# Seven products of half blocks in place of eight for 12 of 22 gate and up pairs of a decoder trunk

## The chip, the cores and the metric

The kernel runs on one NeuronCore of a Trainium2 chip. The metric is the device time of one execution in microseconds. Besides the time, one execution was recorded by the hardware profiler; durations below are from that recording.

## The reference

The reference is a trunk of two layers (DEPTH = 2) on x of 512 tokens by 1024 features, in float32. Each layer does, with an RMSNorm ahead of each step:

```
x = x + 0.5 * swiglu(rmsnorm(x, ffn1_norm), ffn1_w_gate_up, ffn1_w_down)
x = x + mixing(rmsnorm(x, mix_norm))     # sparse attention and a spatial gating unit, gated and merged
x = x + 0.5 * swiglu(rmsnorm(x, ffn2_norm), ffn2_w_gate_up, ffn2_w_down)

def swiglu(h, w_gate_up, w_down):
    g, u = split(h @ w_gate_up, 2)       # 1024 -> 2 * 2816
    return (silu(g) * u) @ w_down        # 2816 -> 1024
```

A last RMSNorm follows. So there are four feed-forward stages (FFN) and two mixing stages. In each FFN the gate and the up matrix have 22 blocks of 128 columns each; a gate block and the up block beside it are called a pair.

## The kernel before

**Number format.** Every product is made of three matmuls on float32r operands: a value is split into hi (rounded by ScalarE, `act(hi, src, Copy)`) and lo = value - hi (VectorE), and hi·hi, hi·lo and lo·hi are summed in PSUM. `split` (line 309) is these two instructions. The activations of a stage lie as xh and xl, eight blocks of 128 features by 512 tokens each; a weight tile of 128 x 1024 holds the eight 128 x 128 blocks of one output block.

**FFN** (`ffn`, line 415). The 22 pairs are worked in chunks of 8, 8 and 6 (`CHUNKS`). For each of the two blocks of a pair, `stage` loads a weight tile of 512 KB, splits it into whi and wlo, and `chain` (line 339) issues 24 matmuls of 512 columns into one PSUM bank: for each k the two with the hi weight, and the one with the lo weight one step later (LAG = 1). So a pair has 48 matmuls. Then VectorE multiplies gate and up by the row factor rbc of the norm, ScalarE does Silu, GpSimd multiplies the two, and the result h is split into two of the R tiles. After each chunk the down projection runs over the chunk: for each of eight output blocks dd a weight tile (1024 or 768 columns), a chain of 3 matmuls per pair, and x is updated by VectorE. In the last chunk `norm_prep` prepares the next stage's xh, xl and the sum of squares (which GpSimd adds up for the blocks below 6).

**Buffers.** A ring of a tag holds n tiles; tile number i of a tag takes place i mod n. Weights go through raw (3 tiles), whi (3) and wlo (2); t has 3 tiles. Gate and up results use six of the eight PSUM banks in turn, down results the banks 6 and 7.

**Order.** Every instruction is first noted with its operands, and `order` (line 206) then lists them for each engine: at each step the engine that is free earliest takes, of the instructions that are ready by a table of costs, the one with the smallest number. Loads and splits of weights are noted with a number smaller by AHEAD = 100, so they go ahead of results. The engines then run their lists strictly in that order, with semaphores for the waits. The table knows nothing of one engine slowing another. All DMAs are issued by SyncE. Since all instructions are issued in one line (L259), rows are told apart by tiles: `b<-xh,whi` is a matmul into a bank with moving operand xh and weight whi.

Of the kernel before, what the change touches and what calls it, by code (L numbers as in the profile page):

```python
# [17 lines left out]
P = 128  # L18
S = 512
# [3 lines left out]
NG = (3 * DEPTH + 1) * KD  # L23
CHUNKS = ((0, 8), (8, 16), (16, 22))
LAG = 1
AHEAD = 100
NEG = -1e30
EPS = 1e-6
# [11 lines left out]
class View:  # L40


    def __init__(self, buf, steps, ids, parts, dtype):
        self.buf, self.steps, self.ids, self.parts, self.dtype = buf, steps, ids, parts, dtype
        self.gen = buf.gen

# [88 lines left out]
class Recorder:  # L135
    def __init__(self, nc):
        self.nc, self.ops, self.rings, self.bias, self.ahead = nc, [], {}, {}, 0
        self.real = {"PE": nc.tensor, "DVE": nc.vector, "ACT": nc.scalar, "POOL": nc.gpsimd, "SP": nc.sync}

    def ring(self, tag, n, cols, dtype=F32, psum=False):  # L140
        self.rings[tag] = [[Buffer(f"{tag}_{k}", cols, dtype, psum) for k in range(n)], 0]

    def tile(self, tag, shape):

        bufs, n = self.rings[tag]
        self.rings[tag][1] += 1
# [10 lines left out]
        v = View(b, tuple(steps), _np.arange(cols).reshape(shape[1:]), (0, P), b.dtype)  # L157
        return v if shape[0] == P else v[0:shape[0]]

    def note(self, engine, op, args, kw):  # L160
        outs = [v for v in [args[0], kw.get("accum_out")] if isinstance(v, View)]
        ins = [v for v in list(args[1:]) + [v for k, v in kw.items() if k != "accum_out"] if isinstance(v, View)]
        i, deps = len(self.ops), set()
        for v, writes in [(v, False) for v in ins] + [(v, True) for v in outs]:
            assert v.gen == v.buf.gen, v.buf.name
# [84 lines left out]
    def issue(self, sbuf, psum):  # L250
        for tag, (bufs, _) in self.rings.items():
            for b in bufs:
                if b.log:
                    b.ap = (psum if b.psum else sbuf).tile([P, b.cols], b.dtype, tag=b.name, name=b.name)
# [8 lines left out]
def trunk(ctx: ExitStack, tc, d):  # L263
# [3 lines left out]
    for tag, n, cols in (("cst", 1, C_END), ("gains", 1, NG), ("pes", 1, 32), ("sgub", 1, DEPTH * 8),  # L267
                         ("ones", 1, P), ("x", 1, KD * S), ("rbc", 1, S), ("eps", 1, 1), ("U", 1, NT * S),
                         ("YA", 1, NT * S), ("GN", 1, NT * 24), ("raw", 3, 1024), ("t", 3, S), ("tb", 2, S),
                         ("ga", 4, S), ("pA", 4, S), ("pB", 4, S), ("pc", 1, 256), ("rcol", 2, 4), ("rhalf", 1, 4), ("ss", 1, 4), ("rv", 1, 4), ("sm4", 8, 4), ("sm8", 4, 8)):  # L270
        rec.ring(tag, n, cols)
    for tag, n, cols in (("whi", 3, 1024), ("wlo", 2, 1024), ("VH", 1, NT * S), ("VL", 1, NT * S), ("kc", 1, P),
                         ("vc", 1, 2 * P), ("diagh", 1, S), ("diagl", 1, S)):
        rec.ring(tag, n, cols, F32R)
    for k in range(24):
        rec.ring(f"R{k}", 1, S, F32R)
# [6 lines left out]
    cst, gains, sgub, ones, rbc, eps = (  # L283
        rec.tile(t, [P, rec.rings[t][0][0].cols]) for t in ("cst", "gains", "sgub", "ones", "rbc", "eps"))
    x = rec.tile("x", [P, KD, S])
    pool.memset(ones, 1.0)
    pool.memset(eps, EPS)

    diag = [rec.tile("diagh", [P, S]), rec.tile("diagl", [P, S])]
    for t in diag:  # L290
        pool.memset(t.bitcast(F32), 0.0)
    ident = cst[:, C_ID:C_ID + P]
# [23 lines left out]
    def stage(src, n, mask=None):  # L316
        if first:
            return first.pop(0)
        return load(src, n, mask)

    def load(src, n, mask=None):
        raw, hi, lo = (rec.tile(t, [P, 1024]) for t in ("raw", "whi", "wlo"))
        rec.ahead = AHEAD
# [26 lines left out]

    st = {}

    def norm_begin(gidx):
        st["g"] = gains[:, gidx * KD:(gidx + 1) * KD]
        st["xh"], st["xl"] = [None] * KD, [None] * KD
        st["s"] = None

    def norm_square(k):

        if st["s"] is None:  # L360
            st["s"] = rec.tile("ga", [P, S])
            act(st["s"], x[:, k, :], AF.Square)
# [46 lines left out]
    def norm_finish(b):  # L409
# [3 lines left out]
        return rcol  # L413

    def ffn(gu, dn, l, gnext):
        norm_finish(7)
        xh, xl = st["xh"], st["xl"]
        nb = 0
        for c0, c1 in CHUNKS:
            hh, hl = [], []  # L420
            for j in range(c0, c1):
                bk = []
                for s in range(2):
                    wh, wl = stage(gu[l, 2 * j + s], 1024)
                    ps = bank(nb % 6, "ps_gu")
                    nb += 1
                    chain(ps, [(wh[:, c], wl[:, c], xh[k], xl[k]) for k, c in enumerate(cols(KD))])
                    bk.append(ps)
                g, u = tt("g"), tt("u")
                vec.tensor_tensor(g, bk[0], rbc, op=ALU.mult)  # L430
                act(g, g, AF.Silu)
                vec.tensor_tensor(u, bk[1], rbc, op=ALU.mult)
                pool.tensor_tensor(u, u, g, op=ALU.mult)
                h = rt(2 * (j % 11), "hh")
                lo = rt(2 * (j % 11) + 1, "hl")
                split(h, lo, u)
                hh.append(h)
                hl.append(lo)
# [72 lines left out]

    def mix(l, gnext):
        rcol = norm_finish(7)
        rhalf = rec.tile("rhalf", [P, 4])
        vec.tensor_scalar(rhalf, rcol, 0.5, None, op0=ALU.mult)
# [386 lines left out]
        def filler():  # L902
            for dd in range(4):
                ga_tile(dd)
# [19 lines left out]
        for dd in range(KD):  # L924
# [27 lines left out]
    for k in range(KD):  # L952
        sync.dma_start(x[:, k, :], d["x"][k])
        if k < 2:
            first.append(load(d["gu1"][0, k], 1024))
    sync.dma_start(cst, d["cst"])
    sync.dma_start(sgub, d["sgub"])
    norm_begin(0)
    for k in range(KD):
# [12 lines left out]
def layout(inp):  # L972
# [88 lines left out]
```

## Time and profile before

| | |
|---|---|
| median of 3 runs | 2201.11 us (2200.51 to 2202.64) |
| profiled execution, device time | 2200.54 us |
| span of its trace | 2198.7 us |
| PE busy | 2172.7 us (99%), 10018 matmuls |
| DVE (VectorE) busy | 1153.1 us (52%) |
| ACT (ScalarE) busy | 886.9 us (40%) |
| POOL (GpSimd) busy | 185.6 us (8%) |
| mean granted TensorE clock | 0.997 of full speed |

Busy PE means matmuls in flight: one is in flight longer than the distance to the next, so the rate is read from the starts of successive matmuls and not from the duration of one. Times in a timeline are from the start of the span. A row of a timeline can hold several like instructions in a row (x2, x4), and its duration is then that of the group. An idle time in brackets names who ended it.

### The profile page before, as it was taken

What the parts mean: (1) busy time and instruction counts of PE and PEld (TensorE: products, weight loads), DVE (VectorE), ACT (ScalarE), POOL (GpSimd) and SP (SyncE); (2) the same over time, 40 slices, a digit from 0 to 9 for tenths busy, and PEclk for the clock granted to TensorE, in tenths of its full rate; (3) what the DMA queues carried; (4) which work ended last, traced back from release to release, by engine and by line L of the source; (5) the groups of instructions that cost most, each with busy time, mean ns of one, the idle gap of its engine ahead of it and who ended that gap; (6) DMA issues with size and microseconds to landing.
All of it is one profiled execution on the core that took longest, in us unless ns stands there. A gap on an engine that the chain in (4) does not pass through costs nothing.

```text
span 2198.7 us, 25769 instructions
## 1 busy us (share of the span) xinstructions
PE 2172.7 (99%) x10018; PEld 1797.2 (82%) x10018; DVE 1153.1 (52%) x1884; ACT 886.9 (40%) x1414; POOL 185.6 (8%) x165
## 2 busy tenths in 40 slices
PE   8999999999999999999999999999999999999998
PEld 6888888788888888888888888877888888888887
DVE  4334336678885533333543343375888755333334
ACT  5323224676653432322432232246766534223223
POOL 2101002010000110100100010110100000101001
PEclk9999999999999999999999999999999999999999
DMA  5333323431113233233333333334211232333322
GB/s 176 96 96 96 96 91 101 137 100 58 58 58 110 93 100 100 96 96 96 95 101 96 96 96 96 89 104 147 90 49 58 77 96 92 94 103 96 96 91 82
DMA packets 61033, 208.95 MB, mean 95 GB/s; under 512 B 7280, under 2 KB 7792, under 8 KB 60912
## 3 DMA queue, kind: packets, MB, share of 16 engines
q1 hardware_dynamic: 60912, 207.32, 30.7%
q8 instruction: 78, 1.28, 0.2%
q14 instruction: 43, 0.35, 0.1%
HBM read 205.19 MB, written 2.10 MB: 94 GB/s over the span
## 4 chain that ended last, share of the span: by engine, by line
PE 93%; DVE 4%; issue 1%; DMA 1%; ACT 1%; SPq 0%; DVEq 0%; ACTq 0%
PE b L259 93%; DVE wlo L259 1%; DVE t L259 1%; DVE R L259 1%; DMA raw<-in_phi_dram 0%; ACT whi L259 0%; DMA x<-in_x_dram 0%; ACT t L259 0%; DVE x L259 0%; DVE xl L259 0%; DVE YA L259 0%; DVE ga L259 0%; DVE U L259 0%; SPq L259 0%; DVE rbc L259 0%
## 5 line engine op out<-in xcount | busy, mean ns | idle before, releaser
L259 DVE TENSOR_TENSOR wlo<-raw,whi 128x1024 fp32r<-128x1024 f32 (+2 forms) x396 | 475.3, 1201 | 752.7 <-issue 560.4
L259 PE MATMUL b<-xh,whi 128*128 128x512 f32 x1920 | 754.4, 393 | 8.4 <-ACT xh L259 7.6
L259 PE MATMUL b<-xl,whi 128*128 128x512 f32 x1920 | 752.8, 392 | 0.1
L259 PE MATMUL b<-xh,wlo 128*128 128x512 f32 x1920 | 715.9, 392 | 4.4 <-DVE wlo L259 4.4
L259 ACT ACTIVATE whi<-raw 128x1024 fp32r<-128x1024 f32 (+3 forms) x396 | 409.7, 1036 | 719.3 <-PE b L259 700.1
L259 PEld LDWEIGHTS b<-xh,whi 128*128 128x128 f32 x1920 | 361.6, 188 | 85.6 <-ACT xh L259 7.6
L259 PEld LDWEIGHTS b<-xh,wlo 128*128 128x128 f32 x1920 | 361.1, 188 | 80.1 <-DVE wlo L259 6.4
L259 PEld LDWEIGHTS b<-xl,whi 128*128 128x128 f32 x1920 | 361.5, 188 | 74.8 <-issue 1.0
L259 PE MATMUL b<-R,whi 128*128 128x512 f32 (+1 forms) x1428 | 418.7, 387 | 0.0
L259 PEld LDWEIGHTS b<-R,whi 128*128 128x128 f32 x1428 | 267.2, 188 | 54.6
L259 PE MATMUL b<-R,wlo 128*128 128x512 f32 (+1 forms) x714 | 259.0, 387 | 0.0
L259 POOL TENSOR_TENSOR t<-t,t 128x512 f32<-128x512 f32 x88 | 113.7, 1292 | 1214.6 <-DVE t L259 1202.5
L259 ACT ACTIVATE R<-t 128x512 fp32r<-128x512 f32 (+3 forms) x152 | 81.4, 551 | 255.3 <-POOL t L259 221.4
L259 DVE TENSOR_TENSOR R<-t,R 128x512 fp32r<-128x512 f32 (+3 forms) x152 | 87.8, 590 | 178.2 <-ACT R L259 177.6
L259 PEld LDWEIGHTS b<-R,wlo 128*128 128x128 f32 x714 | 133.9, 188 | 27.2
L259 DVE TENSOR_TENSOR t<-b,rbc 128x512 f32<-128x512 f32 (+1 forms) x192 | 130.9, 683 | 0.5
L259 PE MATMUL b<-R,R 128*128 128x512 f32 (+3 forms) x416 | 116.3, 357 | 0.0
L259 ACT ACTIVATE t<-t 128x512 f32<-128x512 f32 (+1 forms) x92 | 57.4, 623 | 115.3 <-DVE t L259 115.3
L259 PEld LDWEIGHTS b<-R,R 128*128 128x128 f32 x416 | 74.6, 189 | 12.5
L259 POOL TENSOR_TENSOR ga<-ga,t 128x512 f32<-128x512 f32 x35 | 46.1, 1318 | 434.8 <-ACT t L259 434.5
L259 DVE SCALAR_TENSOR_TENSOR x<-b,x 128x512 f32<-128x512 f32 (+1 forms) x113 | 76.6, 678 | 4.5 <-PE b L259 4.5
L259 ACT ACTIVATE R<-b 128x512 fp32r<-128x512 f32 (+1 forms) x84 | 48.4, 581 | 73.6 <-PE b L259 67.1
(132 smaller groups left out, 1595.1 us busy)
## 6 DMA issues: line engine op xcount, KB each, us to landing
raw<-in_gu_dram SPq DMA_DIRECT2D x176, 512.0 KB, 3.5
raw<-in_dn_dram SPq DMA_DIRECT2D x64, 512.0 KB, 3.5
raw<-in_wA_dram SPq DMA_DIRECT2D x48, 512.0 KB, 3.5
raw<-in_dn_dram SPq DMA_DIRECT2D x32, 384.0 KB, 3.1
raw<-in_phi_dram SPq DMA_DIRECT2D x16, 512.0 KB, 3.9
raw<-in_wo_dram SPq DMA_DIRECT2D x16, 512.0 KB, 3.6
raw<-in_wv_dram SPq DMA_DIRECT2D x8, 512.0 KB, 3.9
raw<-in_wu_dram SPq DMA_DIRECT2D x8, 512.0 KB, 3.8
```

Of the source, the lines that this page charges most:

```text
L259: getattr(self.real[engine], op)(*args, **kw)
```

## The change

A pair is a 1024 x 256 weight matrix times activations of 1024 features by 512 tokens. For 12 of the 22 pairs (11 in the first FFN) it is now cut in halves in all three directions: features 0 to 511 and 512 to 1023, gate and up, tokens 0 to 255 and 256 to 511. Instead of eight products of half blocks it takes seven, of sums of the blocks: weights s1 to s4 are sums of the four weight blocks 11, 12, 21, 22, and activations n1, n2, t3, t4 are sums of the activation blocks (`norm_sums`, made once per FFN after its first pair). A product has 12 matmuls of 256 columns. The results are put together by four VectorE instructions, GpSimd applies the row factor, and Silu is taken with scale -1. The other pairs stay at 48 matmuls of 512 columns. Pairs j with j mod 3 below 2, from 3 (in the first FFN from 4) to 20 are made of seven products.

Also: the weights of a pair come as one tile X of 2048 columns in two DMAs of 512 KB; chunks are 6, 6, 6 and 4 pairs; R has 12 tiles for an FFN instead of 22; t has 4 tiles; the lo weights of an FFN have 3 places; and many tiles of the FFN lie over tiles of the mixing stage (`over`). In the mixing stage ga has 3 places instead of 4, and the ga tiles are made later.

```diff
-CHUNKS = ((0, 8), (8, 16), (16, 22))
+CHUNKS = ((0, 6), (6, 12), (12, 18), (18, 22))
+FIRST, LATER = 4, 3
+def SEVEN(j, begins):
+    return j % 3 < 2 and (FIRST if begins else LATER) <= j < 21
...
+    def over(self, tag, places, cols, dtype=F32):
+        self.rings[tag] = [places, 0, cols, dtype]
...
+            ("Xraw", [(W[0], 0), (W[1], 0)], 2048, F32), ("Fraw", units(W[0], W[1]), 1024, F32),
+            ("S", [(W[2], 0)], 2048, F32), ("T32", [(W[3], 0)], 1024, F32), ...
+            ("Fhi", units(*WH), 1024, F32R), ("Flo", units(*WL), 1024, F32R),
+            ("F22h", halves(V[1])[:2], S, F32R), ("F22l", halves(V[1])[2:], S, F32R),
+            ("raw", units(W[0], W[1])[:3], 1024, F32), ("whi", units(*WH), 1024, F32R), ("wlo", units(*WL)[:2], 1024, F32R),
+            ("U", [(W[2], 0)], 2048, F32), ("pA", halves(W[3]), S, F32), ("pB", halves(W[4]), S, F32),
+            ("ga", halves(W[1])[2:] + [(G, 0)], S, F32), ("diagh", [(WL[2], 0)], S, F32R), ("diagl", [(WL[2], 512)], S, F32R)):
+        rec.over(tag, places, cols, dtype)
...
+    def norm_sums(q):
+        t, xa, xb = rec.tile("T32", [P, 1024]), rec.tile("Txa", [P, S]), rec.tile("Txb", [P, S])
+        act(xa, x[:, q, :], AF.Copy, scale=st["g"][:, q:q + 1])
+        act(xb, x[:, q + 4, :], AF.Copy, scale=st["g"][:, q + 4:q + 5])
+        n1, n2, t3, t4 = (t[:, n * 256:(n + 1) * 256] for n in range(4))
+        vec.tensor_tensor(n1, xa[:, 0:256], xa[:, 256:512], op=ALU.subtract)
...
+        split(st["Th"][q], st["Tl"][q], t)
...
+    def pair_split(X, seven):
...
+        if not seven:
+            part(X[:, 0:1024], ("22", "21"))
+            part(X[:, 1024:2048], ("11", "12"))
...
+        part(X[:, 1024:2048], ("11", "12"))
...
+        vec.tensor_tensor(s4[:, 0:4:3, :], x4[:, 0:3:2, :], x4[:, 1:2, :].to_broadcast([P, 2, 512]), op=ALU.add)
+        vec.tensor_tensor(Sm[:, 512:1024], Sm[:, 0:512], X[:, 1024:1536], op=ALU.add)
+        part(Sm[:, 0:1024], ("s1", "s2"))
+        vec.tensor_tensor(Sm[:, 1024:1536], Sm[:, 512:1024], X[:, 1536:2048], op=ALU.add)
+        part(Sm[:, 1024:2048], ("s4", "s3"))
+        part(X[:, 0:512], ("22",))
...
+    def pair_seven(w):
...
+        A, B, C, D = (next_bank() for _ in range(4))
+        s1, TT = tt("s1")[:, 0:256], rec.tile("TT", [P, 1024])
+        L, R = TT[:, 0:512], TT[:, 512:1024]
+        times(A[:, 0:256], "11", "11")
+        act(s1, A[:, 0:256], AF.Copy)
+        times(B[:, 0:256], "12", "21")
+        times(B[:, 256:512], "s2", "n2")
+        vec.tensor_tensor(half(L), half(B), two(s1), op=ALU.add)
+        times(C[:, 0:256], "s4", "22")
+        times(C[:, 256:512], "s3", "t3")
+        vec.tensor_tensor(half(R), half(C), two(L[:, 256:512]), op=ALU.add)
+        times(D[:, 0:256], "22", "t4")
+        vec.tensor_tensor(L[:, 256:512], D[:, 0:256], R[:, 256:512], op=ALU.add)
+        times(A[:, 256:512], "s1", "n1")
+        vec.tensor_tensor(half(R), half(R), two(A[:, 256:512]), op=ALU.add)
+        for v, r in ((L, rbc[:, 0:256]), (R, rbc[:, 256:512])):
+            pool.tensor_tensor(half(v), half(v), two(r), op=ALU.mult)
+        u = tt("u")
+        t4 = TT.rearrange("p (a b c) -> p a b c", a=2, b=2)
+        act(t4[:, :, 1, :], t4[:, :, 1, :], AF.Silu, scale=-1.0)
+        pool.tensor_tensor(half(u), t4[:, :, 0, :], t4[:, :, 1, :], op=ALU.mult)
+        return u
...
             for j in range(c0, c1):
...
+                seven = SEVEN(j, gnext == 1)
+                w = first.pop() if first else pair_split(pair_load(gu[l, j]), seven)
+                u = (pair_seven if seven else pair_plain)(w)
+                if j == 0:
+                    for q in range(4):
+                        norm_sums(q)
+                h = rt(2 * (j % 6), "hh")
+                lo = rt(2 * (j % 6) + 1, "hl")
                 split(h, lo, u)
...
         def filler():
-            for dd in range(4):
+            for dd in range(3):
                 ga_tile(dd)
...
-            if dd % 2 and dd < 4:
-                ga_tile(dd + 3)
-                ga_tile(dd + 4)
+            if dd % 2:
+                for t in range(dd + 2, min(dd + 4, KD)):
+                    ga_tile(t)
```

## Rows read from the trace of the kernel before

**Rows 1.** The page: busy engines, and the chain that ended last, by engine.
```profile
PE 2172.7 (99%) x10018; PEld 1797.2 (82%) x10018; DVE 1153.1 (52%) x1884; ACT 886.9 (40%) x1414; POOL 185.6 (8%) x165
...
PE 93%; DVE 4%; issue 1%; DMA 1%; ACT 1%; SPq 0%; DVEq 0%; ACTq 0%
```

**Rows 2.** Waits: who for whom, us in total, times, longest.
```profile
PE b L259 <- DVE wlo L259: 5.9, 6, 2.2
```

**Rows 3.** Windows, the middle of an FFN: stretch, its length, each engine's busy us.
```profile
750.00:1060.00 310.00, 310.00 (x1369) 256.80 (x1368) 118.50 (x135) 87.17 (x100) 27.04 (x21) 1.00 0.31 96
```

**Rows 4.** Timeline, PE, last down block: start, us, instruction; 512 columns, then 256.
```profile
2178.02 1.07 PE L259 MATMUL b<-R,whi 128*128 128x512 f32 x4
...
2182.10 0.64 PE L259 MATMUL b<-R,whi 128*128 128x256 f32 x4
...
2184.25 0.52 PE L259 MATMUL b<-R,whi 128*128 128x256 f32 x3
```

**Rows 5.** Timeline, PE, spatial gating: first of nine matmuls of 256 columns, and the next.
```profile
464.15 0.28 PE L259 MATMUL b<-VH,whi 128*128 128x256 f32 x1
...
465.22 0.40 PE L259 MATMUL b<-xh,whi 128*128 128x512 f32 x1
```

**Rows 6.** Groups by form: busy us, mean ns of one, idle before.
```profile
L259 DVE TENSOR_TENSOR wlo<-raw,whi 128x1024 fp32r<-128x1024 f32 x354 | 435.5, 1231 | 695.4 <-issue 550.3 <-PE b L259 115.8 <-ACT whi L259 28.8
...
L259 ACT ACTIVATE whi<-raw 128x1024 fp32r<-128x1024 f32 x354 | 376.4, 1064 | 665.2 <-PE b L259 654.9 <-issue 5.4 <-DMA raw<-in_gu_dram 2.8
...
L259 DVE TENSOR_TENSOR t<-b,rbc 128x512 f32<-128x512 f32 x176 | 120.1, 684 | 0.1
L259 POOL TENSOR_TENSOR t<-t,t 128x512 f32<-128x512 f32 x88 | 113.7, 1292 | 1214.6 <-DVE t L259 1202.5 <-ACT t L259 12.0
...
L259 DVE TENSOR_TENSOR R<-t,R 128x512 fp32r<-128x512 f32 x88 | 60.8, 691 | 175.2 <-ACT R L259 175.2
L259 ACT ACTIVATE R<-t 128x512 fp32r<-128x512 f32 x88 | 55.8, 634 | 221.4 <-POOL t L259 221.4
...
L259 DVE CUSTOM_DVE_ANT_0 pA<-b,cst 128x256 f32<-128x256 f32 x32 | 12.6, 418 | 2.2 <-PE b L259 1.9
```

**Rows 7.** Timeline, POOL and DVE, where they meet in the first FFN.
```profile
33.44 1.30 POOL L259 TENSOR_TENSOR t<-t,t 128x512 f32<-128x512 f32 x1 [12.02 <-ACT t L259]
...
32.00 1.89 DVE L259 TENSOR_TENSOR t<-b,rbc 128x512 f32<-128x512 f32 x3
33.85 1.97 DVE L259 TENSOR_TENSOR wlo<-raw,whi 128x1024 fp32r<-128x1024 f32 x1
```

**Rows 8.** Timeline, POOL, DVE and PE, ahead of PE's longest wait.
```profile
462.02 1.29 POOL L259 TENSOR_TENSOR t<-t,ga 128x512 f32<-128x512 f32 x1 [2.56 <-ACT t L259]
...
462.07 1.78 DVE L259 TENSOR_TENSOR t<-t,t 128x512 f32<-128x512 f32 x1
...
468.48 1.22 DVE L259 TENSOR_TENSOR wlo<-raw,whi 128x1024 fp32r<-128x1024 f32 x1
...
469.75 0.80 PE L259 MATMUL b<-xh,wlo 128*128 128x512 f32 x1 [2.21 <-DVE wlo L259]
```

**Rows 9.** Windows, just behind that wait (PEclk is the figure ahead of the last two).
```profile
470.00:475.00 5.00, 5.00 (x21) 4.16 (x22) 4.07 (x9) 1.76 (x3) 1.71 (x1) 0.74 0.29 86
```

**Rows 10.** Timeline, PE and ACT: the last hi matmuls of a tile, its overwriting.
```profile
108.85 0.62 PE L259 MATMUL b<-R,whi 128*128 128x512 f32 x2
...
109.50 1.06 ACT L259 ACTIVATE whi<-raw 128x1024 fp32r<-128x1024 f32 x1 [3.42 <-PE b L259]
```

**Rows 11.** Timeline, DVE, one output block of an FFN's last down projection.
```profile
358.43 1.34 DVE L259 SCALAR_TENSOR_TENSOR xl<-x,gains,xh 128x512 fp32r<-128x512 f32 x1 [1.31 <-ACT xh L259]
359.69 0.95 DVE L259 TENSOR_TENSOR wlo<-raw,whi 128x768 fp32r<-128x768 f32 x1
360.56 0.68 DVE L259 SCALAR_TENSOR_TENSOR x<-b,x 128x512 f32<-128x512 f32 x1
```

More of the change, by code (lines that the diff above doesn't have):

```diff
@@ L250, in issue @@
     def issue(self, sbuf, psum):
-        for tag, (bufs, _) in self.rings.items():
-            for b in bufs:
-                if b.log:
+        for places, *_ in self.rings.values():
+            for b, _ in places:
+                if b.log and b.ap is None:
                     b.ap = (psum if b.psum else sbuf).tile([P, b.cols], b.dtype, tag=b.name, name=b.name)
@@ L274, in trunk, with units @@
         rec.ring(tag, n, cols, F32R)
+    W = [Buffer(f"W{k}", 2048, F32, False) for k in range(5)]
+    WH = [Buffer(f"WH{k}", 1024, F32R, False) for k in range(3)]
+    WL = [Buffer(f"WL{k}", 1024, F32R, False) for k in range(3)]
+    RB = [Buffer(f"RB{k}", 1024, F32R, False) for k in range(12)]
+    V = [rec.rings[t][0][0][0] for t in ("VH", "VL")]
+    G = Buffer("G", S, F32, False)
+    YB = Buffer("YB", 2048, F32, False)
+    rec.over("YA", [(YB, 0)], 2048)
+    def units(*bufs):
+        return [(b, c) for b in bufs for c in range(0, b.cols, 1024)]
@@ L275, in trunk @@
     for k in range(24):
-        rec.ring(f"R{k}", 1, S, F32R)
+        rec.over(f"R{k}", [(RB[k // 2], k % 2 * 512)], S, F32R)
+    for k, place in enumerate([(b, 0) for b in RB[6:]] + units(V[0])):
+        rec.over(("Th", "Tl")[k // 4] + str(k % 4), [place], 1024, F32R)
+    rec.over("TT", units(YB), 1024)
     for k in range(KD):
@@ L283, in trunk @@
     cst, gains, sgub, ones, rbc, eps = (
-        rec.tile(t, [P, rec.rings[t][0][0].cols]) for t in ("cst", "gains", "sgub", "ones", "rbc", "eps"))
+        rec.tile(t, [P, rec.rings[t][2]]) for t in ("cst", "gains", "sgub", "ones", "rbc", "eps"))
     x = rec.tile("x", [P, KD, S])
@@ L316, in stage @@
     def stage(src, n, mask=None):
-        if first:
-            return first.pop(0)
         return load(src, n, mask)
     def load(src, n, mask=None):
-        raw, hi, lo = (rec.tile(t, [P, 1024]) for t in ("raw", "whi", "wlo"))
+        raw, hi, lo = (rec.tile(t, [P, 1024]) for t in st["rings"])
         rec.ahead = AHEAD
@@ new lines, in trunk, with next_bank, pair_plain @@
+    nb = [0]
+    def next_bank():
+        nb[0] += 1
+        return bank(nb[0] % 6, "ps_gu")
+    def pair_plain(w):
+        out = []
+        for p, q in (("21", "22"), ("11", "12")):
+            ps = next_bank()
+            ops = []
+            for k in range(KD):
+                h, lo = w[p if k < 4 else q]
+                c = slice(k % 4 * P, (k % 4 + 1) * P)
+                ops.append((h[:, c], lo[:, c], st["xh"][k], st["xl"][k]))
+            chain(ps, ops)
+            out.append(ps)
+        g, u = tt("g"), tt("u")
+        vec.tensor_tensor(g, out[0], rbc, op=ALU.mult)
+        act(g, g, AF.Silu)
+        vec.tensor_tensor(u, out[1], rbc, op=ALU.mult)
+        pool.tensor_tensor(u, u, g, op=ALU.mult)
+        return u
@@ new lines, in pair_seven, with times, two, half @@
+    def pair_seven(w):
+        xh, xl, Th, Tl = st["xh"], st["xl"], st["Th"], st["Tl"]
+        def times(o, key, kind):
+            h, lo = w[key]
+            ops = []
+            for k in range(4):
+                cc = slice(k * P, (k + 1) * P)
+                yh, yl, n = {"11": (xh[k], xl[k], 0), "21": (xh[k + 4], xl[k + 4], 0),
+                             "22": (xh[k + 4], xl[k + 4], 1), "n1": (Th[k], Tl[k], 0), "n2": (Th[k], Tl[k], 1),
+                             "t3": (Th[k], Tl[k], 2), "t4": (Th[k], Tl[k], 3)}[kind]
+                t = slice(n * 256, (n + 1) * 256)
+                ops.append((h[:, cc], lo[:, cc], yh[:, t], yl[:, t]))
+            chain(o, ops)
+        def two(v):
+            return v.unsqueeze(1).to_broadcast([P, 2, 256])
+        def half(v):
+            return v.rearrange("p (a c) -> p a c", a=2)
+        A, B, C, D = (next_bank() for _ in range(4))
[19 more added lines that the diff above has]
+        pool.tensor_tensor(half(u), t4[:, :, 0, :], t4[:, :, 1, :], op=ALU.mult)
+        return u
@@ L512, in mix @@
     def mix(l, gnext):
+        st["rings"] = ("raw", "whi", "wlo")
         rcol = norm_finish(7)
+        diag = [rec.tile("diagh", [P, S]), rec.tile("diagl", [P, S])]
+        for t in diag:
+            pool.memset(t.bitcast(F32), 0.0)
         rhalf = rec.tile("rhalf", [P, 4])
```

107 lines of the change are left out of this document (61 added, 46 removed).

## The prediction, made before the changed kernel ran

> **What bounds the kernel now.** I read the busy shares and the chain first, then PE's waits, then the rate of the matmuls, then the groups of VectorE and GpSimd, and last the places where these two meet. PE is busy for 99% of the span and 93% of the chain is PE; VectorE has 52%, GpSimd 8% [rows 1]. In the middle of an FFN PE never stops: 310.00 us busy in 310 us, at full clock, with the DMA engines at 0.31 [rows 3]. So the count of matmuls times the distance between two starts is the time. For 512 columns the distance is (2182.10 - 2178.02) / 18 = 226.7 ns, for 256 columns in the same kind of chain (2184.25 - 2182.10) / 18 = 119.4 ns [rows 4]; a short run elsewhere gives 1.07 / 9 = 119 ns [rows 5]. Half the columns cost 53% of the time, not 50%.
>
> **PE's part.** A plain pair is 48 x 226.7 ns = 10.88 us, a pair of seven products 7 x 12 = 84 matmuls x 119.4 ns = 10.03 us. That saves 0.85 us a pair. There are 11 + 12 + 12 + 12 = 47 such pairs: 40.0 us. An eighth of the products goes, but more than a third of that is paid back by the shorter matmuls. Down projections and the mixing stages keep their matmuls.
>
> **VectorE's and GpSimd's part.** From the group means [rows 6], a pair of seven costs VectorE: lo splits 3 x 1.231 + 0.691 = 4.38; weight sums 1.231 + 2 x 0.691 = 2.61; putting results together from PSUM 3 x 0.684 + 0.418 = 2.47; the lo of h 0.691; together 10.16 us. That is as long as the pair takes on PE. A plain pair costs 2 x 1.231 + 2 x 0.684 + 0.691 = 4.52. The pattern is two of seven and one plain: VectorE 24.84 us, PE 2 x 10.03 + 10.88 = 30.94 us (three plain pairs before: 32.65 and 13.56). GpSimd has three products in a pair of seven and one in a plain one: 7 x 1.292 = 9.04 us in the three (a broadcast factor is taken at the price of a plain one). ScalarE, with 3 x 1.064 + 4 x about 0.6 in a pair of seven and 2 x 1.064 + 2 x 0.634 in a plain one, stays below half of PE. Since a chunk holds at most two such threes and then 8 x 18 x 0.2267 = 33 us of down projection, VectorE can catch up there.
>
> VectorE and GpSimd aren't free of each other. A GpSimd product ran from 33.44 to 34.74; the VectorE split of two SBUF operands that started at 33.85 took 1.97 us instead of 1.231 and ended 1.08 us after GpSimd did. The three VectorE products with a PSUM operand beside it took 1.89 us, not longer than three of 0.684 [rows 7]. So what counts is whether VectorE reads two SBUF operands: of its 24.84 us these are 18.53, the PSUM ones 6.31. The Trainium skill, page "SBUF — State Buffer", section "SBUF: two separate sides", calls the port pair of the two engines an exclusive lock: a VectorE instruction with two SBUF inputs and a GpSimd instruction that reads SBUF exclude each other, and whoever started first has the port for its whole instruction. By that rule the trace agrees in both cases above.
>
> With such exclusion the shared part is 18.53 + 9.04 = 27.57 us in 30.94, which fits; if VectorE's list, being in order, stood still through all of GpSimd's work, it would be 24.84 + 9.04 = 33.88, which doesn't. I expect something near the first: a third or more of GpSimd's time beside PSUM instructions and idle time.
>
> **Where PE will wait.** A tile of hi or lo weights has three places, a pair of seven uses three, so the tile (s1, s2) of the second of two successive pairs takes the place of the first one's, and s1 is the first one's last product. ScalarE starts to overwrite a place about 0.42 us after the start of its last hi matmul (109.50 against 109.08, the second of the two of [rows 10]). The last hi matmul starts three steps, 0.36 us, before the next pair does, so counted from that pair's start: hi from 0.06 to 1.12, lo to 1.12 + 1.231 = 2.35. s2 is wanted by the third product: hi after 24 steps, 2.87 us, lo after 28, 3.35 us. That leaves 1.0 us. In the same microseconds VectorE has the last addition of the pair before (0.684), and GpSimd its row factors. One GpSimd product in front (1.292) makes lo late by 0.3 us; with a VectorE sum (1.231) in progress as well by about 1.5. Bounds 0 and 1.5 us a place; I take 0.4, nearer to the case of one product in front, since the lists put splits ahead of results. There are 6 such places in an FFN and 5 in the first: 23 x 0.4 = 9.2 us. Behind a late lo on VectorE's list stand the additions that free the PSUM banks; the next pair needs its first freed bank only at its fourth product, 4.3 us in, which covers them. What covers all this gone, a wait grows: the 2.21 us wait of PE came from just such a GpSimd product, 462.02 to 463.31, that held a VectorE addition to 1.78 us and with it the split that PE wanted [rows 8].
>
> **Joins of the FFNs.** The last chunk has four pairs now: an output block takes PE 12 x 0.2267 = 2.72 us. VectorE has for it 1.34 + 0.69 + 0.68 = 2.71 us (the 0.95 us split is 512 columns wide now) [rows 11]; before, PE took 4.08. So xl of the last blocks may come late; PE has chains of the next stage to fill with, as long as weights are split. At the beginning the four activation sums cost VectorE 4 x (4 x 0.418 + 1.231) = 11.6 us, between the first pair and the fourth: with 3 x 4.52 and 7.0 us of weights for the first seven that is 32.2 of 32.65 us. The last pair's h comes 1.292 + 0.634 + 0.691 = 2.6 us after its u, and with four pairs in a chunk it is wanted after 8 x 0.2267 = 1.8 us; the next output block, on the other bank, can go first. Bounds 0 to 3 us an FFN; I take 1, near the covered case: 4 us.
>
> **Nothing, with its cover.** Loads: the same bytes, at 0.31 of the DMA engines; two X tiles of 1 MB cover 20 us. Four more chunk ends put 32 updates of 0.68 us on VectorE, beside 4.08 us of PE each. The R tiles come round after six pairs, but a first h is written 10 us after the down projection that reads the old one. The overlaid tiles change hands at stage ends where their last readers are long done, except the weight places, which have three tiles on either side. In the mixing stage three ga tiles instead of four and four t tiles instead of three: from -2 to +3 us, taken as 0. If one of these covers fails, it costs a wait of the size of a load or a split at a join, 1 to 4 us each time.
>
> **The sum.** Profiled execution 2200.5 us (span 2198.7 and 1.8 around it) - 40.0 + 9.2 + 4 = 2173.7; the median of the runs is 0.6 us above the profiled one, so 2174. About 0.2% is what a measurement of this kernel can tell from no change; 2174 is 1.2% faster.
>
> **The rivals.** (1) All waits are covered: 2200.5 - 40.0 = 2161. For it: PE lost nothing in the FFN before [rows 3], and all its waits for a lo split together were 5.9 us [rows 2]. Against it: VectorE had 118 of 310 us there and will have four fifths. 10%.
> (2) The s2 tile is late by a GpSimd product more at each place: 23 x 1.3 = 30 us instead of 9.2, and 2 us more at the joins: 2195, range 2184 to 2196. 9%.
> (3) Slower: VectorE stands still for GpSimd's work and becomes the bound. It decides from the point where less than 33.88 - 32.65 = 1.23 us of GpSimd's 9.04 lie beside PSUM work or idle time. Price at no overlap at all: 47 / 2 threes x 1.23 = 29 us, 2229; and a wait of 2.2 us was followed by 5 us at a granted clock of 0.74, between the levels of 2.4 and 1.2 GHz, which loses another 1.3 us each time [rows 9]. For it: VectorE's list is in order and most of it is two SBUF operands. Against it: the down projections give time to catch up, and a GpSimd product usually starts behind a PSUM addition. 9%.
> (4) The change doesn't save what it says: the 119.4 ns are from 36 matmuls, and if 84 in a row took 10.88 / 84 = 129.5 ns, nothing would be gained and the waits of 13 us paid: 2214. For it only that each short matmul still has a weight load of its own; against it two places with the same distance. 4%.
>
> **How the numbers follow.** My forecast, 2162 to 2184, has 64%. Faster by over 0.2% (below 2196.7): 64 + 10 + 9 = 83%. Within 0.2%: 4% for what lies between (2) and (3). Slower: 9 + 4 = 13%. The range of 8 in 10 takes in half of (1) and all of (2) but its edge: 2160 to 2198; the bounds of the unknown costs alone (0 to 34, 0 to 12, -2 to 3) would give 2158 to 2210.
>
> **What would show it.** PE's matmuls of 256 columns start 119 to 120 ns apart; 47 x 48 = 2256 of 512 columns go and 47 x 84 = 3948 of 256 come. VectorE's busy time rises by 47 x 5.64 + 46 + 22 = 333 us to near 1490, GpSimd's by 47 x 2.58 = 121 us. PE's waits are for DVE's lo tiles, at the third product of every second pair of seven, below 1 us each. VectorE's two-operand splits beside a GpSimd product take up to 2 us. It is wrong if PE waits elsewhere (for banks, for R), if waits recur in plain pairs, or if the granted clock falls inside an FFN.

## The result and the profile after

The changed kernel takes 2179.32 us (median of 4 runs, 2178.57 to 2181.16) against 2201.11 us for the kernel before (median of 3; a fourth, slow run of 2483.97 us is left out), a ratio of 0.990 [0.988, 0.992]. The forecast was 2174, the range 2160 to 2198. The time is 5 us off, but two terms of the sum were wrong in opposite directions. They show once the span is cut into stages (from the matmul that broadcasts one norm's factor to that of the next; the last FFN ends with the first broadcast of the last norm):

| us | four FFNs | two mixing stages | start and tail | span |
|---|---|---|---|---|
| before | 1425.8 | 733.3 | 39.6 | 2198.7 |
| after | 1392.2 | 744.2 | 40.7 | 2177.2 |
| difference | -33.6 | +10.9 | +1.1 | -21.5 |

The border between two stages is not the same work in every kernel: the order on PE puts some matmuls of the next stage ahead of the broadcast. After runs 3623 matmuls in its mixing stages and before 3616; seven of 512 columns are 1.6 us. At the same count of matmuls the mixing stages lost 9.2 us and not 10.9. Ten such matmuls, 2.3 us, left the FFNs, three of them to the start, so the FFNs saved 31.3 and not 33.6. The whole time isn't touched by this.

First the page of after: the span, the busy times, and the chain of waits by engine [rows 1].

```profile
span 2177.2 us, 30080 instructions
PE 2142.5 (98%) x11704; PEld 1849.4 (85%) x11704; DVE 1523.9 (70%) x2357; ACT 1012.5 (47%) x1635; POOL 381.7 (18%) x261
PE 92%; DVE 5%; ACT 1%; issue 1%; DMA 0%; SPq 0%; DVEq 0%; ACTq 0%
```

PE still has 92% of the chain. VectorE rose by 371 us where 333 were forecast, GpSimd by 196 where 121 were. Yet PE's waits, second, for lo tiles (`WL`, the old `wlo`) went only from 5.9 us [rows 2] to 8.2, and all seven of them lie in the mixing stages (columns: total, times, longest):

```profile
PE b L276 <- ACT xh L276: 8.2, 1, 8.2
PE b L276 <- DVE WL L276: 8.2, 7, 2.2
PE b L276 <- ACT WH L276: 3.6, 7, 1.2
PE b L276 <- DVE W L276: 2.5, 2, 1.4
```

Third, the stretch of an FFN that was shown of before [rows 3]. PE is as full as it was, at full clock, with VectorE at 204 us instead of 118.5 and GpSimd at 77 instead of 27. Columns: busy us of PE, PEld, DVE, ACT, POOL, then granted clock, DMA share, GB/s.

```profile
750.00:1060.00 310.00, 310.00 (x1843) 277.37 (x1842) 204.00 (x241) 113.65 (x147) 77.06 (x45) 1.00 0.32 97
```

Since PE doesn't stop there, the distance between matmuls is again the price. These are successive starts in a pair of seven, with the border between two successive pairs at 150.00:

```profile
150.00 0.28 PE L276 MATMUL b<-xh,WH 128*128 128x256 f32 x1
150.12 0.28 PE L276 MATMUL b<-xl,WH 128*128 128x256 f32 x1
150.24 0.28 PE L276 MATMUL b<-xh,WH 128*128 128x256 f32 x1
```

The median over all 4128 such neighbours of 256 columns in the trace is 120.0 ns, against 119.4 in [rows 4]. So a pair of seven is 84 x 0.120 = 10.08 us, a pair saves 0.80 us, and 47 pairs save 37.6 us. The FFNs kept 33.6 of these by their length, 31.3 at the same count of matmuls.

The same border on VectorE, GpSimd and ScalarE, where the prediction put its wait for s2:

```profile
149.96 1.06 ACT L276 ACTIVATE WH<-W 128x1024 fp32r<-128x1024 f32 x1 [1.44 <-PE b L276]
150.29 3.56 POOL L276 TENSOR_TENSOR YB<-YB,rbc 128x512 f32<-128x512 f32 x2 [7.09 <-DVE YB L276]
150.31 0.69 DVE L276 TENSOR_TENSOR YB<-YB,b 128x512 f32<-128x512 f32 x1
151.05 1.62 DVE L276 TENSOR_TENSOR WL<-W,WH 128x1024 fp32r<-128x1024 f32 x1
152.88 0.64 PE L276 MATMUL b<-RB,WH 128*128 128x256 f32 x4
153.36 0.28 PE L276 MATMUL b<-RB,WL 128*128 128x256 f32 x1
```

Here `WL<-W,WH` at 151.05 is lo of (s1, s2). It was lengthened from 1.23 [rows 6] to 1.62 us by the GpSimd products beside it, a lengthening that was forecast, and ended at 152.67. Its first reader on PE started at 153.36. There was 0.7 us to spare and no wait. At 22 of the 23 places of this kind lo ended 0.67 to 1.08 us before its first reader started, at one 0.07 us.

Last the groups of VectorE and GpSimd in which the extra busy time lies (busy, mean ns, then idle time before them):

```profile
L276 DVE TENSOR_TENSOR WL<-W,WH 128x1024 fp32r<-128x1024 f32 x337 | 428.4, 1273 | 134.0 <-ACT WH L276 56.0 <-PE b L276 42.9 <-issue 32.1
L276 DVE TENSOR_TENSOR W<-W 128x1024 f32<-128x1024 f32 x47 | 75.1, 1599 | 1.4 <-DMA W<-in_gu_dram 0.3
L276 DVE TENSOR_TENSOR YB<-b,YB 128x512 f32<-128x512 f32 x47 | 32.2, 686 | 13.2 <-PE b L276 12.0
L276 POOL TENSOR_TENSOR YB<-YB,rbc 128x512 f32<-128x512 f32 x94 | 169.2, 1817 | 671.2 <-DVE YB L276 671.2
L276 POOL TENSOR_TENSOR t<-YB 128x512 f32<-128x512 f32 x47 | 69.6, 1481 | 36.2 <-ACT YB L276 36.2
```

Instructions with two SBUF operands grew on both engines: the weight sums from 1231 to 1599 ns, GpSimd's products from 1292 to 1817. The VectorE addition that reads PSUM (`b`) stayed at 686 against 684.

### The profile page after: what moved, and what is told of

The parts are those of the page before. It is cut to its first block, busy times and chain, and to the rows that moved or that the text cites. A ratio compares the mean times of both kernels' runs of the same rounds, so it can differ in the third digit from the quotient of the medians.

```text
span 2177.2 us, 30080 instructions
## 1 busy us (share of the span) xinstructions
PE 2142.5 (98%) x11704; PEld 1849.4 (85%) x11704; DVE 1523.9 (70%) x2357; ACT 1012.5 (47%) x1635; POOL 381.7 (18%) x261
## 4 chain that ended last, share of the span: by engine, by line
PE 92%; DVE 5%; ACT 1%; issue 1%; DMA 0%; SPq 0%; DVEq 0%; ACTq 0%
PE b L276 92%; DVE WL L276 1%; DVE RB L276 1%; DVE t L276 1%; DVE W L276 1%; DVE x L276 1%; DVE xl L276 1%; ACT WH L276 0%; ACT t L276 0%; DMA x<-in_x_dram 0%; ACT RB L276 0%; DVE YB L276 0%; ACT xh L276 0%; ACT W L276 0%; DVE sm L276 0%
## 5 line engine op out<-in xcount | busy, mean ns | idle before, releaser
L276 ACT ACTIVATE WH<-W 128x1024 fp32r<-128x1024 f32 (+4 forms) x475 | 463.7, 978 | 648.5 <-PE b L276 572.6
L276 DVE TENSOR_TENSOR WL<-W,WH 128x1024 fp32r<-128x1024 f32 (+4 forms) x475 | 553.0, 1166 | 204.1 <-ACT WH L276 112.2
L276 PE MATMUL b<-xh,WH 128*128 128x512 f32 (+1 forms) x1732 | 614.8, 359 | 11.3 <-ACT xh L276 8.2
L276 PE MATMUL b<-xl,WH 128*128 128x512 f32 (+1 forms) x1732 | 615.0, 359 | 0.6 <-DVE xl L276 0.4
L276 PE MATMUL b<-xh,WL 128*128 128x512 f32 (+1 forms) x1732 | 576.7, 359 | 6.8 <-DVE WL L276 6.8
L276 PE MATMUL b<-RB,WH 128*128 128x512 f32 (+2 forms) x2270 | 579.5, 349 | 0.4
L276 PEld LDWEIGHTS b<-RB,WH 128*128 128x128 f32 x2270 | 398.0, 189 | 57.2 <-DVE x L276 2.1
L276 PE MATMUL b<-RB,WL 128*128 128x512 f32 (+1 forms) x1276 | 391.5, 341 | 0.0
L276 PEld LDWEIGHTS b<-xh,WH 128*128 128x128 f32 x1732 | 329.5, 190 | 59.6 <-ACT xh L276 8.2
L276 PEld LDWEIGHTS b<-xl,WH 128*128 128x128 f32 x1732 | 329.2, 190 | 47.5 <-DVE xl L276 2.2
L276 POOL TENSOR_TENSOR YB<-YB,rbc 128x512 f32<-128x512 f32 x94 | 169.2, 1817 | 671.2 <-DVE YB L276 671.2
```

Source lines behind the costliest of these rows:

```text
L276: getattr(self.real[engine], op)(*args, **kw)
```

## The experiments

All times are medians beside the kernel before on the same chip; "mixing" is the sum of the two mixing stages (733.3 us before, 744.2 after), "FFNs" that of the four (1425.8 and 1392.2).

**e1: no pair of seven.** Buffers, chunks and mixing stage as changed.

```diff
 def SEVEN(j, begins):
-    return j % 3 < 2 and (FIRST if begins else LATER) <= j < 21
+    return False
```

> The changed kernel with no pair of seven products (all 22 pairs plain, the activation sums left out), everything else as changed. In the changed kernel the four FFNs save 32 us of the 38 that the matmuls promise, and the two mixing stages lose 11 us (367 to 373 us and 366 to 371 us between the norm broadcasts). Theory: the 11 us come from the mixing stage's own edits (three ga places, later ga tiles, shared buffers, another list), so they stay: the time is 2201 + 11 + 2 at the joins = 2214, ratio to the kernel before 1.004 to 1.007. Rival: the mixing stages suffer from VectorE's and GpSimd's work for the pairs of seven at their borders; then the loss goes with them, and the time is 2201 to 2204, ratio 1.000 to 1.0015.

Measured: 2213.88 us (2212.36 to 2216.14), ratio 1.005 [1.004, 1.007]; mixing 741.2, FFNs 1428.6. So what surrounds the sevens costs 11 us by itself: 7.9 in the mixing stages and 2.8 in the FFNs. The mixing stages run ten matmuls more than before here (3626), so at the same count they lost 5.5. The sevens then take 36.4 us off the FFNs, out of 37.6, but with them the mixing stages are 3.0 us longer: in after the granted clock was 0.50 for 10.2 us of these stages, in e1 and in before for 3.4 us, and 6.8 us more at half the clock cost an estimated 3.4 us.

**e2: pairs of seven without a plain one between** (71 pairs).

```diff
-    return j % 3 < 2 and (FIRST if begins else LATER) <= j < 21
+    return (FIRST if begins else LATER) <= j < 21
```

> All pairs from j = 3 (4 in the first FFN) to 20 by seven products, 71 instead of 47. If PE stays the bound, 24 pairs more save 24 x 0.84 = 20 us: 2159, ratio 0.981. Theory: VectorE and GpSimd become the bound where no plain pair lies between: a pair of seven has 7.7 us of VectorE instructions with two SBUF operands and 3 x 1.3 to 1.8 us of GpSimd that exclude them, 11.6 to 13 us against 10.08 us on PE, so 71 pairs lose 1.5 to 3 us each less what the down projections absorb: 2200 to 2290, slower than the changed kernel, and PE waits for lo tiles in the middle of the FFNs.

Measured: 2233.25 us (2229.38 to 2236.04), ratio 1.014 [1.013, 1.016]. More of the cheaper pairs make it slower than before: PE's list waits for lo tiles, and the FFNs take 1447.3 us where 1428.6 - 71 x 0.80 = 1371.8 would be PE's own. The wait in e2's summary, then one place in its timeline. Of these 52.7 us, 44.6 in 37 waits lie before matmuls of pairs of seven, the rest in the mixing stages, as in after. Not all of the 75 us by which the FFNs are too long is waiting: the granted clock fell to 0.50 for 34 us of the FFNs, against 3.4 us in after, which by half of 34 us is an estimated 17 us more.

```profile
PE b L276 <- DVE WL L276: 52.7, 44, 2.7
```

```profile
144.05 2.97 POOL L276 TENSOR_TENSOR YB<-YB,rbc 128x512 f32<-128x512 f32 x2 [5.63 <-DVE YB L276]
144.08 0.69 DVE L276 TENSOR_TENSOR YB<-YB,b 128x512 f32<-128x512 f32 x1
144.68 1.22 DVE L276 TENSOR_TENSOR VL<-W,VL 128x512 fp32r<-128x512 f32 x1
145.83 2.28 DVE L276 TENSOR_TENSOR WL<-W,WH 128x1024 fp32r<-128x1024 f32 x1
148.16 0.39 PE L276 MATMUL b<-RB,WL 128*128 128x256 f32 x1 [2.73 <-DVE WL L276]
```

The addition from PSUM beside GpSimd's first product takes its usual 0.69 us. The next two VectorE instructions, with two SBUF operands, take 1.22 and 2.28 instead of 0.69 and 1.23, and PE waits 2.73 us for the second. GpSimd's two products take 2.97 together, not 2 x 1.29: they wait for VectorE as well. The Trainium skill, page "SBUF — State Buffer", section "SBUF: two separate sides", says that whichever of the two starts first has the port pair for its whole instruction and the other blocks. By that rule the trace agrees, both ways round.

**e10: as e2, without GpSimd's row factors.** They are replaced by a scaled copy on ScalarE (the row factor is left out there), so GpSimd has one product a pair instead of three and the weight work of VectorE is the same.

```diff
-            pool.tensor_tensor(half(v), half(v), two(r), op=ALU.mult)
+            act(v, v, AF.Copy, scale=2.0 ** -7)
```

> All pairs from 3 to 20 by seven products, as in the run that took 2233 us, but GpSimd's two row factor products of each such pair are replaced by two ScalarE copies with a constant factor (the row factor itself is left out there). Theory: VectorE's splits were late because GpSimd's row factors excluded them at the border of two pairs (a split took 2.28 us instead of 1.23 and PE waited 2.73); without them VectorE's 10.2 us of a pair just fit the 10.08 us of PE: 2160 to 2178, and PE's waits for lo tiles fall from 52.7 us to below 15. Rival: VectorE's own load and the place that (s1, s2) shares are the cause: 2215 to 2235, waits above 35 us.

Measured: 2173.52 us (2171.87 to 2175.37), ratio 0.987 [0.986, 0.989]; 60 us less than e2. In e10's waits:

```profile
PE b L276 <- DVE WL L276: 16.0, 24, 2.2
```

The 16.0 us just miss the expected bound of 15; 8.1 of them lie in the mixing stages, so that the 44.6 us of e2's FFNs fell to 7.9. The time is as the exclusion has it. VectorE's mean for a 1024-column split fell from 1370 to 1270 ns, and the mean granted clock of the span rose from 0.987 to 0.995. So VectorE's own 10.2 us a pair nearly fit into PE's 10.08, and the loss of e2 is made by GpSimd's 142 products beside them and by the lower clock in the wake of the waits. That is rival (3)'s mechanism, real, and past its point in e2.

**e3: s2 wanted one product earlier.**

```diff
-        times(B[:, 0:256], "12", "21")
         times(B[:, 256:512], "s2", "n2")
+        times(B[:, 0:256], "12", "21")
```

> In a pair of seven the product with s2 stands second instead of third, so its weights are wanted 12 x 0.12 = 1.44 us earlier. In the changed kernel the lo of (s1, s2) of the second of two successive pairs ended at 152.67 and was wanted at 153.36, 0.7 us to spare, and no PE wait was seen. Theory: the place of (s1, s2) is free only with the last product of the pair before, so lo is now late by 1.44 - 0.7 = 0.7 us at 23 places: 2179 + 16 = 2195, and PE waits for lo tiles inside the FFNs. Rival: the list puts another product in front or splits earlier, and nothing is lost: 2176 to 2182.

Measured: 2185.28 us (2183.28 to 2186.50), ratio 0.992 [0.990, 0.994]: 6 us above after, between the two forecasts (2195, and 2176 to 2182); the FFNs take 6.7 us more (1398.9). The large loss that the theory expected did not come. The same border in e3:

```profile
151.59 1.62 DVE L276 TENSOR_TENSOR WL<-W,WH 128x1024 fp32r<-128x1024 f32 x1
151.97 0.64 PE L276 MATMUL b<-RB,WH 128*128 128x256 f32 x4
152.45 0.28 PE L276 MATMUL b<-xh,WH 128*128 128x256 f32 x1
...
152.81 0.28 PE L276 MATMUL b<-xl,WH 128*128 128x256 f32 x1
152.93 0.28 PE L276 MATMUL b<-xh,WL 128*128 128x256 f32 x1
153.26 0.38 PE L276 MATMUL b<-RB,WL 128*128 128x256 f32 x1
```

Four matmuls of the s2 product (`RB,WH`) run, then five of another product (`xh`, `xl`) are put in front of the first one that needs lo at 153.26. The order written for PE moves work into the hole, so a product brought 1.44 us forward costs 0.2 us of waiting here. Over the 23 places such holes, and 1.7 us for a second stretch of lower clock in the FFNs, make up most of the 6.7 us. Instructions of a chain aren't bound to stand together.

**e4: the chunk of four pairs first instead of last.**

```diff
-CHUNKS = ((0, 6), (6, 12), (12, 18), (18, 22))
+CHUNKS = ((0, 4), (4, 10), (10, 16), (16, 22))
```

> Chunks of 4, 6, 6, 6 pairs instead of 6, 6, 6, 4: an output block of the last down projection takes PE 18 x 0.2267 = 4.08 us instead of 2.72, against 2.7 us of VectorE. Theory: the waits of PE at the joins (1.6 us at 366, 1.3 us and 1.6 us of lower clock at 1091, 0.9 us at 1445) come from VectorE falling behind in the four wide chunk: 3 to 5 us go, 2175, ratio 0.988. Rival: they come from what the next stage does first (shared weight places, the activation sums), and nothing changes: 2178 to 2181.

Measured: 2186.00 us (2184.41 to 2187.32), ratio 0.993 [0.991, 0.994]. Missed: it is slower than after by 6 us. The stall at the FFN's end did go. In after, PE stands at the end of the first FFN for the sum of squares and runs on at 367.53:

```profile
365.74 0.39 PE L276 MATMUL b<-xh,WH 128*128 128x512 f32 x1
367.53 0.83 PE L276 MATMUL b<-ones,W 128*128 128x1 f32 x6 [1.41 <-DVE W L276]
```

But now the first chunk of four pairs ends at pair 3, which outside the first FFN is one of seven products, and its h is late for the down projection. In e4, three times:

```profile
781.09 0.39 PE L276 MATMUL b<-RB,WL 128*128 128x512 f32 x1
783.02 1.22 PE L276 MATMUL b<-RB,WH 128*128 128x512 f32 x3 [1.55 <-ACT RB L276]
```

Behind the chunks of six pairs, which end with the pairs 9 and 15 and so with a pair of seven too, PE waited 0.1 us at most. That the longer down blocks cover the late h there is argued from this and was not tested by itself.

**e8: e4's chunks, and the pattern shifted so that each chunk ends with a plain pair** (48 pairs of seven).

```diff
-    return j % 3 < 2 and (FIRST if begins else LATER) <= j < 21
+    return j % 3 > 0 and 4 <= j < 21
```

> Chunks of 4, 6, 6, 6 pairs as in the run with the wide last chunk, but the pairs of seven moved by one (j mod 3 above 0, from 4 to 20, 48 in all), so that every chunk ends with a plain pair. In the run with the wide last chunk the waits at the joins at 366 and 1091 us were gone, but PE waited 1.7 us three times behind the chunk that ended with a pair of seven (781, 1136, 1862 us), whose h comes late. Theory: both are now gone: 2180 - 3 to 5 at the joins - 0.8 for the pair more: 2175, ratio 0.987 to 0.988. Rival: the loss of that run was elsewhere (a first chunk of four leaves VectorE less time): 2183 or more, ratio 0.991 or more.

Measured: 2172.71 us (2171.92 to 2173.08), ratio 0.987 [0.985, 0.988]; FFNs 1382.0, 10.2 less than after, of which 0.8 is the one pair more. But the mixing stages are 3.5 us longer than after's (747.7): 17 matmuls more run in them, 3.9 us, that the FFNs no longer have. At the same count of matmuls the FFNs gain 5.5 us besides the pair. Where after waited 1.41 us, e8 doesn't:

```profile
365.46 0.39 PE L276 MATMUL b<-xl,WH 128*128 128x512 f32 x1
365.69 0.95 PE L276 MATMUL b<-ones,W 128*128 128x1 f32 x8
```

**e5: four ga tiles and their old order, three t tiles.**

```diff
-    ("t", 4, S)
+    ("t", 3, S)
-    G = Buffer("G", S, F32, False)
+    G = Buffer("G", 2 * S, F32, False)
-    ("ga", halves(W[1])[2:] + [(G, 0)], S, F32)
+    ("ga", halves(W[1])[2:] + [(G, 0), (G, S)], S, F32)
-            for dd in range(3):
+            for dd in range(4):
...
-                for t in range(dd + 2, min(dd + 4, KD)):
-                    ga_tile(t)
+                ga_tile(dd + 3)
+                ga_tile(dd + 4)
```

> The changed kernel with ga in four places and the ga tiles made as before (four in the filler, two after the output blocks 1 and 3), paid for by three t tiles instead of four. Theory: the third of the mixing stage's loss that lies behind the attention (1.6 us of wait at its end, 0.7 to 1.1 us more in the tail, a layer) comes from the missing ga tile, which was a filler: 4 to 6 us go, 2174, ratio 0.988. Rival: it comes from the overlaid buffers, which are as changed here: 2177 to 2182.

Measured: 2173.37 us (2170.32 to 2175.17), ratio 0.987 [0.985, 0.988]; mixing 736.6, 7.6 less than after. At the end of attention, after stands (first row), while e5 has matmuls to run (second fence):

```profile
641.84 0.50 PE L276 MATMUL b<-xh,WL 128*128 128x512 f32 x1 [1.25 <-DVE WL L276]
```

```profile
640.12 0.40 PE L276 MATMUL b<-VH,WH 128*128 128x512 f32 x1
```

**e6: three t tiles alone**, the first line of e5's edit.

> The changed kernel with three t tiles as before, nothing else; the control for the run with four ga tiles. If the fourth t tile helps nothing: 2177 to 2182, ratio 0.989 to 0.991. If the pairs of seven need it (each holds two t tiles until its h is split), PE waits come up inside the FFNs: 47 x 0.2 = 9 us, 2188. If its other list is what brought the 1.3 us wait for a hi tile 7.5 us behind the spatial gating, that wait goes in both layers: 2175.

Measured: 2178.68 us (2176.44 to 2179.74), ratio 0.989 [0.988, 0.991]; mixing 741.2, 3.0 less than after. Whether the whole time moves can't be told by this. The wait for a hi tile (in after the one that ended at 459.55) goes, and a stretch of lower clock is shorter; the wait at the end of attention (641.84 in after) stays. So the latter comes from the ga tiles, their number and order together, and of e5's 7.6 us some 4.6 are theirs.

**e7: the sine product of the rotary step on VectorE instead of GpSimd.**

```diff
-            pool.tensor_tensor(rot, rot, sinr, op=ALU.mult)
+            vec.tensor_tensor(rot, rot, sinr, op=ALU.mult)
```

> The changed kernel with the sine product of the rotary step on VectorE instead of GpSimd (six a layer). Theory: PE's waits of 1.3 and 2.3 us in each mixing stage (458 and 460 us in the first) come from a GpSimd product that held VectorE's addition (1.79 us instead of 0.69) and with it the splits behind it; without GpSimd there both go, and with them the 2 us of lower clock that sometimes follow: 2 x 3.6 to 2 x 5.6 us, 2169 to 2173, ratio 0.985 to 0.987. Rival: VectorE was late anyway, six more products of 0.69 us on it make it later: 2180 to 2185.

Measured: 2172.49 us (2172.02 to 2172.76), ratio 0.987 [0.985, 0.988]; mixing 737.4, 6.8 less than after. What happens in after, in the rotary step:

```profile
454.80 1.75 POOL L276 TENSOR_TENSOR t<-t,G 128x512 f32<-128x512 f32 x1 [2.10 <-ACT t L276]
455.31 1.79 DVE L276 TENSOR_TENSOR t<-t,t 128x512 f32<-128x512 f32 x1
457.13 1.29 ACT L276 ACTIVATE RB<-t 64x512 fp32r<-64x512 f32 x2 [2.41 <-DVE t L276]
458.44 1.06 ACT L276 ACTIVATE WH<-W 128x1024 fp32r<-128x1024 f32 x1
459.55 0.50 PE L276 MATMUL b<-xh,WH 128*128 128x512 f32 x1 [1.15 <-ACT WH L276]
462.90 0.80 PE L276 MATMUL b<-xh,WL 128*128 128x512 f32 x1 [2.15 <-DVE WL L276]
462.20:468.90 6.70, 6.00 (x16) 4.84 (x17) 4.49 (x8) 2.65 (x5) 1.71 (x1) 0.50 0.21 64
```

A GpSimd product holds VectorE's sum to 1.79 us; ScalarE waits 2.41 us for it with RB at the head of its list; the hi of the next weight tile stands behind that on ScalarE, PE waits for it, and 3 us later for its lo. The last row, a window, shows PE's granted clock from the last part of that wait on: 0.50, the 1.2 GHz level. In e7 the first wait is gone and the second is 1.53 us, where the theory had both go, with the clock at 1.00 over the same step (last row):

```profile
462.16 0.50 PE L276 MATMUL b<-xh,WL 128*128 128x512 f32 x1 [1.53 <-DVE WL L276]
455.00:470.00 15.00, 13.47 (x72) 11.13 (x72) 14.61 (x27) 10.59 (x17) 0.00 (x0) 1.00 0.19 58
```

The clock stayed at 1.00 through both mixing stages of e7, where after had 10.2 us at 0.50, which by half of that cost it an estimated 5.1 us; PE's idle time fell by 3.9 us. Both together are more than the 6.8 us, and what took the difference was not separated.

**e9: e8, e5 and e7 together.**

> The three edits that gained, together: chunks of 4, 6, 6, 6 with the pairs of seven moved by one, four ga places with three t tiles, and the rotary sine product on VectorE. If the gains are of separate waits, they add up: 2179.3 - 6.6 - 5.9 - 6.8 = 2160, ratio 0.981. The runs with three t tiles and with VectorE's rotary product share the 1.3 us wait in each mixing stage that they took away, so 2160 to 2164. Rival: the same PE slack is won twice, and no more than the best single one plus 3 us comes out: 2169.

Measured: 2163.11 us (2161.89 to 2163.81), ratio 0.982 [0.981, 0.984], inside the range for gains that are partly shared. This beats both kernels; FFNs 1382.9, mixing 737.4. By length the mixing stages gain no more than by e5 or e7 alone, but they run the 17 matmuls more that came with e8's chunks; against e8 they gain 10.3 us, where e5 and e7 gained 7.6 and 6.8.

The mixing stages compared. PE idle is their length less PE's busy time; the matmuls are counted by their starts:

| | us | matmuls | PE idle, us | us at clock 0.50 | longer than before at the same count, us |
|---|---|---|---|---|---|
| before | 733.4 | 3616 | 9.1 | 3.4 | |
| after | 744.2 | 3623 | 13.9 | 10.2 | 9.2 |
| e1 | 741.2 | 3626 | 13.5 | 3.4 | 5.5 |
| e5 | 736.6 | 3623 | 9.1 | 6.8 | 1.6 |
| e6 | 741.1 | 3623 | 12.0 | 6.8 | 6.1 |
| e7 | 737.4 | 3623 | 10.0 | 0 | 2.4 |
| e8 | 747.7 | 3640 | 13.7 | 10.2 | 8.9 |
| e9 | 737.4 | 3640 | 8.6 | 0 | -1.4 |

The windows of before, then of after (a matmul in flight at a border counts on both sides of it):

```profile
380.16:747.29 367.13, 362.70 (x1809) 300.73 (x1808) 275.72 (x580) 215.99 (x434) 17.64 (x14) 1.00 0.29 88
1468.98:1835.27 366.29, 361.63 (x1809) 299.71 (x1808) 275.70 (x580) 215.95 (x434) 17.42 (x13) 1.00 0.28 87
372.37:745.70 373.33, 366.69 (x1816) 302.89 (x1815) 284.18 (x593) 220.96 (x442) 18.26 (x14) 0.99 0.28 88
1452.21:1823.09 370.88, 363.64 (x1810) 300.71 (x1809) 283.99 (x594) 220.46 (x441) 17.93 (x13) 1.00 0.27 87
```

## Why the prediction was right in its time and wrong in its terms

- **PE's saving** (40.0): right in kind, 37.6 by the distance of 120.0 ns. Rival (4) is excluded: 3948 matmuls of 256 columns hold the distance that 36 of them showed.
- **The wait for s2** (9.2): this step failed. No place waited. The step put a whole GpSimd product (1.29 us), and sometimes a VectorE sum, in front of lo. In the border shown GpSimd's product began 0.76 us before lo, beside VectorE's addition from PSUM, and lo was lengthened by 0.39 us (1.62 instead of 1.23), so it still came 0.7 us early. e3 shows besides that where less time is left, the order on PE puts other matmuls ahead: I priced a late operand as if PE's next matmuls were fixed. After two pairs of seven comes a plain one, and VectorE catches up; without it (e2) the FFNs wait for lo 37 times.
- **The joins** (4): 37.6 - 33.6 = 4.0 us were lost in the FFNs by their length, 6.3 at the same count of matmuls, inside the bounds of 0 to 12. By e1, 2.8 us by length are there without pairs of seven. The place is the one named, the last chunk of four pairs: PE waits 1.41 and 1.13 us for the sum of squares, and behind the second wait the clock was 0.50 for 3.4 us. e8 takes nearly all of it away (0.7 us are left at the same count), by two edits that only work together (e4).
- **The mixing stages** (0, bounds -2 to +3): this step failed by 10.9 us, 9.2 at the same count of matmuls, outside its bounds. The bounds came from counting places of tiles. Of the 9.2, PE's idle time is 4.8 us (13.9 instead of 9.1) and the lower clock an estimated 3.4 us. e1 shows 5.5 of it without any pair of seven. e5 shows that with fewer and later ga tiles PE has no filler at the end of attention. In the rotary step e6 and e7 both remove the wait of 1.15 us. That GpSimd's product holds VectorE's sum there is not what is new: the sum took 1.78 us in before [rows 8] and in e6 too, without that wait. In after the product itself was longer as well, 1.75 us instead of 1.29 (1.30 in e6), in the order that came with the fourth t tile; why that order makes PE wait is argued and not shown. The prediction put the 2.21 us wait of [rows 8] down to that product; with the product on VectorE, 1.53 of 2.15 us are left in e7, so the hold made up only a part of such a wait. e9 has no loss left in these stages: 4.1 us more by length, but 24 matmuls more than before, 5.4 us.
- **Rival (3)**: wrong for this pattern, right as a mechanism. Its point of decision was put as GpSimd's time that doesn't lie beside PSUM work or idle time. e2 passed that point and was slower than before, and e10 removed the products and the loss. That the 1.4% of e2 are near the rival's 1.3% is chance: the rival's price was for 47 pairs with plain ones between, e2 has 71 without.
- **Rival (1)** missed by 18 us, though its condition was met where the prediction looked for the loss, at the pairs of seven: the loss was at the joins and in the mixing stages.
- **VectorE's and GpSimd's busy times** were forecast too low, by 38 and 75 us; instructions that meet on the two engines took longer than alone (1599 instead of 1231 ns, 1817 instead of 1292). No pair of seven made PE wait for this.

With the terms as measured the profiled execution is 2200.5 - 37.6 + 0 + 4.0 + 10.9 + 1.1 (start and tail) = 2178.9, and it was 2179.2. The 9.2 us that didn't come covered the 10.9 that weren't forecast: the time was right in part by luck.

## What to carry to other kernels

When tiles of one stage are laid over those of another, price the other stage too: here a quarter of the gain of a smaller matmul count (9.2 of 37.6 us) was lost in stages whose arithmetic wasn't touched, through a filler tile fewer, a new order of their instructions, and the lower clock behind longer waits. Before comparing stages, count their matmuls, since the order may have moved some across the border. Before giving GpSimd work beside a busy VectorE, count the instructions with two SBUF operands on both; those compete, PSUM ones don't, and a pause in the pattern (one plain pair in three) decided between a gain and a loss. At a join behind a short chunk, the last piece should be the one with the shortest tail.

## What the runs showed of the hardware

- The exclusion runs both ways: a GpSimd product of 1.29 us took 1.82 us on average over 94, while VectorE's splits beside it rose from 1.23 to 1.62 (after) or 2.28 us (e2).
- With a weight load for each matmul, 256-column matmuls started 120.0 ns apart over whole pairs, 53% of the distance for 512 columns.
- A wait of PE of 1 to 2 us was followed by a stretch at granted clock 0.50 in some places and not in others. In after the clock was 0.50 from 462.1 to 469.0, beginning within the wait that ended at 462.90; and behind a wait of 1.13 us that ended at 1092.14 it was 0.50 as in the first row below. In before the same wait of 2.21 us was followed by lower clock in the first layer [rows 9] and not in the second (last two rows):

```profile
1093.60:1097.00 3.40, 3.40 (x9) 2.66 (x8) 1.41 (x6) 3.37 (x5) 0.00 (x0) 0.50 0.24 93
1558.80 0.50 PE L259 MATMUL b<-xh,wlo 128*128 128x512 f32 x1 [2.21 <-DVE wlo L259]
1557.00:1567.00 10.00, 8.20 (x44) 6.84 (x45) 9.81 (x17) 6.17 (x11) 1.72 (x1) 1.00 0.16 45
```

What decides was not tested.
